# Shift rows summed before the mean square, 128-wide early products, and sliding-window values as float32 products at two column positions

## The chip, the core and the metric

The kernel runs on one core of a Trainium2 chip. A core has five engines that each work through their own list of instructions in order: TensorE (PE; its weight loads are listed apart as PEld), VectorE (DVE), ScalarE (ACT), GpSimd (POOL) and SyncE (SP, which here only issues DMAs). They meet through semaphores. TensorE writes to PSUM banks, the others read those and write to SBUF. The metric is the device time of one execution in microseconds. The program is one launch.

## The reference

One layer of a decoder trunk over 512 tokens of width 1024, in float32, with conditioning by a vector `c`:

```python
mod = silu(c) @ w_ada + b_ada                     # six rows: shift, scale, gate, twice
h = rmsnorm(x, norm1_g) * (1 + scale1) + shift1
qa, ka, va, qd, kd, vd, ga, gd = split(h @ w_in)
out_a = sliding_window_attention(qa, ka, va)      # 8 heads of 64, 2 key/value heads, window 128, sinks, ALiBi
out_d = diff_attention(qd, kd, vd)                # 4 heads, two softmax maps each, values 128 wide
merged = sigmoid(ga) * (out_a @ w_branch_swa) + sigmoid(gd) * (out_d @ w_branch_diff)
x = x + gate1 * (merged @ w_out)
h2 = rmsnorm(x, norm2_g) * (1 + scale2) + shift2
x = x + gate2 * conv_ffn(h2)                      # 2816 wide, causal conv of width 3, GELU, gate
return rmsnorm(x, final_g)
```

In the sliding-window attention the 512 queries are four blocks of 128, and a block sees its own block of keys and the one before. The probabilities of a head (a block of queries by up to 256 keys) are multiplied with the values of that head's key/value head.

## The kernel before

**Products in split form.** Most products are made from operands that are split into a high part in the type float32r and a low part, the remainder. `mm3` (line 105) issues three products: high by high, high by low and low by high. A split costs one copy on ScalarE (the high part) and one subtraction on VectorE (the low part); `split` (line 101) does it for weights, and `evac` (line 374) for results that leave PSUM. Products in plain float32 occur too: the column sums of squares, the sums of one modulation block, and the transposes and warming products against an identity or ones. A plain float32 product shows as two weight loads and two matmul records in the profile, a transpose as one of each.

**The start (lines 165 to 345).** VectorE, ScalarE, TensorE and GpSimd run in the order written (`manual_schedule`). SP loads x transposed in four pieces, then for each of eight blocks k of 128 features two blocks of modulation weights (`adaw[k]`, filled by `load_ada`, line 170) and a block of the input projection (`w0[k]`). For k = 0 the block in place j = 0 is laid out for TensorE (`w_ada_0`, the scale of the first 128 features); all others are rows for VectorE. `keep_warm` (line 205) issues products whose result nobody reads. The order for the first block is:

- ScalarE squares x in four pieces; VectorE adds the halves of a piece; `sums` (line 262) makes four products of a piece with a column of ones, `NB` = 48 columns wide, into one PSUM bank that a product with zeros has cleared.
- `rstd_start` (line 136) takes the mean square `ms` on VectorE and a power on GpSimd; `head_mod` (line 249) makes eight products for the scale, also `NB` wide; `mod_rows(0, 1)` sums the shift rows on VectorE (a multiplication with a running sum, line 232); `rstd_end` finishes `rst`, one over the root.
- two warming products, the high split of `w0[0]`, `mod_end` (line 234) on ScalarE, four transposes that spread `rst` (line 285), four warming products, and then x is scaled (line 292), h is formed (line 298) and the first products of the projection follow.

For each further block, 24 products of 512 columns run while VectorE and ScalarE make the next block's h.

**Sliding-window attention (lines 472 to 552).** The heads are taken in four pairs, head i with head i + 4; the two heads of a pair use different key/value heads. TensorE keeps its order as written; the other engines are ordered by a planner. For a pair there are `swa_scores` (two calls, products of 64 rows, the two heads in the two halves of the array's rows), `swa_softmax` (exponentials on ScalarE, scaling by one over the sum on VectorE, line 522), `swa_transpose` (line 524, one call for each head: seven transposes into two PSUM banks of the tag "t", each evacuated as a high and a low part) and `swa_values` (line 539). The value product is full width: `va` is held as high and low parts, with each key/value head's 64 columns in its own half of 128 and zeros in the other, so both heads add up into one bank `o`. `turn_va` (line 402) makes `va` from the transposed projection, after GpSimd has cleared it.

Between these calls `fill(n)` (line 431) issues n steps of other work for TensorE, the projections of later tiles; one step is three products of 512 columns. The counts stand in `SWA_FILL` and `DIFF_FILL`. A function handed to `after(n, ...)` runs n steps later. While the steps run, rows of the modulation for later use are loaded and summed on VectorE (`ada_rows`, line 679).

**Differential attention (lines 584 to 673)** follows, block by block for four heads, with `diff_values(h)` (line 643) one block into the next head, and for the last head after a `fill(1)` at line 792. `diff_values` reads the split transposed maps `aTh` and `aTl`; statistics and the scaling of its result come 10 and 26 steps later. Merge, output projection, MLP and final norm come behind, and no edit touches them.

Of the kernel before, what the change touches and what calls it, by code (L numbers as in the profile page):

```python
# [8 lines left out]
F32 = mybir.dt.float32  # L9
F32R = mybir.dt.float32r  # L10
# [4 lines left out]
P = 128  # L15
# [3 lines left out]
NT = S // P  # L19
# [24 lines left out]
def kernel(  # L44
# [60 lines left out]
    def mm3(o, lh, ll, rh, rl, start, stop):  # L105
        nc.tensor.matmul(o, lh, rh, start=start, stop=False)
        nc.tensor.matmul(o, lh, rl, start=False, stop=False)
        nc.tensor.matmul(o, ll, rh, start=False, stop=stop)
# [27 lines left out]
    def rstd_start(ssq, n, d, wpool, plus=None):  # L136
        ms = wpool.tile([P, n], F32, tag="rs_a", bufs=3, name="ms")
        if plus is None:
            nc.vector.tensor_scalar(ms, ssq, 1.0 / d, EPS, ALU.mult, ALU.add)  # L139
        else:  # L140
            nc.vector.scalar_tensor_tensor(ms, ssq, 1.0 / d, plus, ALU.mult, ALU.add)
        r0 = wpool.tile([P, n], F32, tag="rs_c", bufs=3, name="r0")
        nc.gpsimd.tensor_tensor(r0, ms, mhalf[:, :n], ALU.pow)  # L143
        return ms, r0
# [25 lines left out]
    def load_ada(k):  # L170
        if k % 4 < 2:
            adaw[k] = big.tile([P, 2, D], F32, tag=("outh", "outl")[k % 4], name=f"adaw{k}")
        else:
            adaw[k] = pp.tile([P, 2, D], F32, tag="adaw", bufs=2, name=f"adaw{k}")
        for j in range(2):
            src = w_ada_t[(1 - j) * D + k * P : (1 - j) * D + (k + 1) * P, :] if k or j else w_ada_0
            nc.sync.dma_start(adaw[k][:, j], src)

# [26 lines left out]
    def keep_warm(n):  # L205
        for i in range(n):
            nc.tensor.matmul(acc[5][:, :P], ones, ones, start=True, stop=True)
# [22 lines left out]
    def mod_rows(k, j):  # L230
        a = adaw[k][:, j]
        nc.vector.tensor_tensor_reduce(a, a, csb, 1.0, 0.0, ALU.mult, ALU.add, mods[k][:, 2 + j : 3 + j])
# [11 lines left out]
    def split_lo(k):  # L244
        nc.vector.tensor_sub(wts[k][1], w0[k], wts[k][0].bitcast(F32))

    NB = 48

    def head_mod():
        for a in range(KT):  # L250
# [3 lines left out]
            )  # L254

    stat = acc[6][:, : NT * NB].rearrange("p (t n) -> p t n", n=NB)
    zeros = pp.tile([P, NT * NB], F32, name="zeros")
    nc.gpsimd.memset(zeros, 0.0)
    keep_warm(2)
    nc.tensor.matmul(acc[6][:, : NT * NB], ones, zeros, start=True, stop=True)  # L260

    def sums(p):
        for t in range(NT):
            nc.tensor.matmul(
                stat[:, t], sqs[p][:, t * P : (t + 1) * P], ones[:, :NB], start=False, stop=True,
                skip_group_check=True,
            )

    sqs = [pp.tile([P, 2 * S], F32, tag="sq", bufs=4, name=f"sq{p}") for p in range(KT // 2)]
    for p in range(KT // 2):  # L270
        nc.scalar.activation(sqs[p], xT[:, p], AF.Square)
        if p == 1:
            nc.scalar.copy(csb[:, S:], acc[1])
        nc.vector.tensor_add(sqs[p][:, :S], sqs[p][:, :S], sqs[p][:, S:])
        sums(p)
    ms, r0 = rstd_start(stat[:, :, 0], NT, D, pp)
    head_mod()
    mod_rows(0, 1)
    rst = pp.tile([P, NT], F32, name="rst")
    rstd_end(rst, ms, r0, NT, pp)  # L280
    keep_warm(2)
    split_hi(0)
    mod_end(0, [acc[3][:, 0:1], mods[0][:, 3:4]])
    for t in range(NT):
# [74 lines left out]
    ddf = cpool.tile([P, 512], F32, name="ddf")  # L359
    nc.gpsimd.iota(ddf, [[1, 512]], base=-384, channel_multiplier=-1, allow_small_or_imprecise_dtypes=True)  # L360
    nc.gpsimd.affine_select(ddf, ddf, [[-1, 512]], ALU.is_ge, NEG, base=384, channel_multiplier=1)
    va = big.tile([P, 2, 4, 2 * P], F32R, tag="kvB", name="va")
    nc.gpsimd.memset(va.bitcast(F32), 0.0)
    man.close()
    p1.close()

# [7 lines left out]
    def evac(hi, lo, src, scale=None):  # L374
        if scale is None:
            nc.scalar.copy(hi, src)
            nc.vector.tensor_sub(lo, src, hi.bitcast(F32))
        else:
            nc.scalar.activation(hi, src, AF.Copy, scale=scale)
            nc.vector.scalar_tensor_tensor(lo, src, scale, hi.bitcast(F32), ALU.mult, ALU.subtract)  # L380
# [21 lines left out]
    def turn_va():  # L402
        pv = tbank("pva")
        for t in range(NT):
            nc.tensor.transpose(pv[:, t * P : (t + 1) * P], vaT[:, t * P : (t + 1) * P], ident)
        pv3 = pv.rearrange("p (t d) -> p t d", t=NT)
        for a, cc in ((0, 0), (64, 192)):
            evac(va[:, 0, :, cc : cc + 64], va[:, 1, :, cc : cc + 64], pv3[:, :, a : a + 64])

    with tc.issue_after(tiles[KT - 1, 0].ins):  # L410

# [19 lines left out]
    def fill(n):  # L431
        for _ in range(n):
            if not current:
                prefetch(2 if tick[0] else 1)
                if loaded:
                    wts, run = loaded.pop(0)
                    current.append(run(wts))
                    if tick[0]:
                        prefetch()
            if tick[0] in (2, 7):  # L440
                prefetch(1 if tick[0] == 2 else 2)
            if current:
                try:
                    next(current[0])
                except StopIteration:
                    current.clear()
            for e in list(later):
                e[0] -= 1
                if e[0] <= 0:
                    later.remove(e)  # L450
                    e[1]()
            tick[0] += 1
            if tick[0] >= ADA_START and tick[0] % ADA_EVERY == 0:
                next(ada, None)
# [68 lines left out]

    def swa_transpose(i, j):
        c = pairs[i]
        ph = ap.tile([P, 1024], F32R, tag="aTh", bufs=2, name=f"pTh{i}_{j}")
        pl = ap.tile([P, 1024], F32R, tag="aTl", bufs=2, name=f"pTl{i}_{j}")
        for b in range(2):
            wb = 512 if b == 0 else 384
            tp = tbank(f"tp{i}_{j}_{b}")  # L530
            for m in range(wb // P):
                kb, n = 2 * b + m // 2, 2 * b + m // 2 + m % 2
                off = (kb - max(0, n - 1)) * P
                nc.tensor.transpose(tp[:, m * P : (m + 1) * P], c.sb[n][:, j, off : off + P], ident)
            with tc.high_priority(offset=HP):
                evac(ph[:, b * 512 : b * 512 + wb], pl[:, b * 512 : b * 512 + wb], tp[:, :wb])
        c.pT.append((ph, pl))

    def swa_values(i):
        o = vbank(f"oa{i}")  # L540
        for j in range(2):
            ph, pl = pairs[i].pT[j]
            vs = slice(P * j, P * j + P)
            for kb in (0, 2, 1, 3):
                w = P if kb == 3 else 2 * P
                mm3(
                    o[:, kb * P : kb * P + w],
                    va[:, 0, kb, vs], va[:, 1, kb, vs],
                    ph[:, kb * 256 : kb * 256 + w], pl[:, kb * 256 : kb * 256 + w],
                    j == 0 and kb == 0, j == 1 and kb == 3,  # L550
                )
        evac(outa[0][:, i], outa[1][:, i], o)

# [235 lines left out]
            fill(DIFF_FILL[3])  # L789
    for j in range(6, KT):  # L790
        add_gate_a(j)
    fill(1)
    diff_values(DIFF_HEADS - 1)
    while units or loaded or current:
        fill(1)
# [935 lines left out]
```

## Time and profile before

| | |
|---|---|
| runs | 703.93, 704.18, 707.34 us (median 704.18) |
| profiled execution | 704.71 us, span 702.9 us |
| mean granted TensorE clock | 0.989 |
| busy: TensorE, weight loads | 684.5 us (97%), 601.4 us (86%) |
| busy: VectorE, ScalarE, GpSimd | 568.2 us (81%), 377.1 us (54%), 75.3 us (11%) |
| bytes moved by DMA | 119.68 MB, 170 GB/s |

All times are counted from the start of the span. The start runs to about 62 us, sliding-window attention from there to about 130, differential attention to about 231; the MLP's main products begin near 400. In a group row, "x24" is a count, then come the busy time, the mean length in ns, and the engine's idle time ahead of the group with what ended it. "A <- B" among the waits is an engine and line that waited, and the instruction that let it go on. The granted clock is 1.00 or 0.50 of full speed in this trace. Matmul records overlap, so a busy TensorE is not one at its peak rate: where a price is wanted, the distance from one start to the next is used.

### The profile page before, as it was taken

How to read it: one execution, taken by the hardware profiler on the slowest of the kernel's cores; microseconds unless marked ns; L12 is line 12 of the kernel's file. 1: busy time of each engine (PE TensorE's matmuls, PEld its weight loads, DVE VectorE, ACT ScalarE, POOL GpSimd, SP SyncE). 2: the span in 40 equal slices, each digit the busy share in tenths (PEclk: the TensorE clock that was granted, in tenths of full speed). 3: DMA queues.
4: the chain of work that ended last, by engine and by line, in shares of the span. 5: the costliest groups of instructions: out<-in, count | busy, mean ns of one | idle time of the engine just before them, and what ended most of it. 6: DMA issues, size and time to landing. Idle time of an engine off the chain costs nothing. (4 is left out here: it accounts for less than half of the span.)

```text
span 702.9 us, 11006 instructions
## 1 busy us (share of the span) xinstructions
PE 684.5 (97%) x4155; PEld 601.4 (86%) x4155; DVE 568.2 (81%) x1046; ACT 377.1 (54%) x662; POOL 75.3 (11%) x83
## 2 busy tenths in 40 slices
PE   8999899999998999999999999999999999999994
PEld 8887678877886788888889999999999998888873
DVE  3888999687787467673589898888888999979995
ACT  4656565454554243332478566655565665655663
POOL 3100000000010000000030111111101003431200
PEclk8999999999999999999999999999999999999998
DMA  9943453435364366239526888788777648996803
GB/s 356 397 162 112 152 152 120 122 120 160 110 180 150 123 210 213 102 102 269 180 57 153 197 196 204 171 223 191 185 182 194 151 166 195 197 204 178 154 1 120
DMA packets 71077, 119.68 MB, mean 170 GB/s; under 512 B 3952, under 2 KB 47728, under 8 KB 71024
## 3 DMA queue, kind: packets, MB, share of 16 engines
q1 hardware_dynamic: 52960, 95.04, 40.9%
q0 software_dynamic: 17776, 23.60, 20.4%
q8 instruction: 32, 0.52, 0.3%
q10 hardware_dynamic: 288, 0.34, 0.1%
q14 instruction: 21, 0.17, 0.1%
HBM read 116.87 MB, written 2.10 MB: 169 GB/s over the span
## 5 line engine op out<-in xcount | busy, mean ns | idle before, releaser
L1062 PE MATMUL up<-t,m_whi 128*128 128x256 f32 x528 | 96.1, 283 | 0.0
L1062 PEld LDWEIGHTS up<-t,m_whi 128*128 128x128 f32 x528 | 82.3, 192 | 0.0
L1062 PE MATMUL up<-t,m_wlo 128*128 128x256 f32 x264 | 74.7, 283 | 0.1
L1062 PE MATMUL up<-bh,p_wlo 128*128 128x256 f32 x232 | 65.7, 284 | 0.7 <-DVE p_wlo L1005 0.7
L1062 PE MATMUL up<-bh,p_whi 128*128 128x256 f32 x232 | 65.6, 283 | 0.0
L1062 PE MATMUL up<-bl,p_whi 128*128 128x256 f32 x232 | 65.6, 283 | 0.0
L684 DVE CUSTOM_DVE_ANT_0 ra<-ra,csb 128x1024 f32<-128x1024 f32 x32 | 39.1, 1223 | 24.3 <-DMA ra<-in_w_ada_t_dram 24.3
L1062 PEld LDWEIGHTS up<-t,m_wlo 128*128 128x128 f32 x264 | 50.6, 192 | 0.3 <-DVE m_wlo L1005 0.3
L1062 PEld LDWEIGHTS up<-bh,p_wlo 128*128 128x128 f32 x232 | 44.4, 192 | 1.1 <-DVE p_wlo L1005 1.1
L143 POOL TENSOR_TENSOR r<-ms,mhalf 128x1 f32<-128x1 f32 (+1 forms) x13 | 12.7, 979 | 303.2 <-DVE ms L139 227.0
L1062 PEld LDWEIGHTS up<-bh,p_whi 128*128 128x128 f32 x232 | 44.5, 192 | 0.0
L1062 PEld LDWEIGHTS up<-bl,p_whi 128*128 128x128 f32 x232 | 44.5, 192 | 0.0
L973 POOL DMA_DIRECT2D s<-in_w_up_dram x21 | 27.1, 1364 | 155.9 <-DMA s<-in_w_up_dram 110.9
L1005 DVE TENSOR_TENSOR m_wlo<-s,m_whi 128x1024 fp32r<-128x1024 f32 x31 | 37.8, 1219 | 2.0 <-ACT m_whi L1001 2.0
L1001 ACT CAST m_whi<-s 128x1024 fp32r<-128x1024 f32 x31 | 32.4, 1046 | 9.3 <-DVE s L995 6.0
L623 ACT ACTIVATE sd<-sd,dmx 128x128 f32<-128x128 f32 (+3 forms) x32 | 17.8, 557 | 30.8 <-DVE dmx L621 24.6
L1062 PE MATMUL up<-t,p_whi 128*128 128x256 f32 x176 | 32.2, 283 | 0.0
L1062 PEld LDWEIGHTS up<-t,p_whi 128*128 128x128 f32 x176 | 27.4, 192 | 0.2 <-issue 0.2
L1069 ACT ACTIVATE gT<-a,cols 128x512 f32<-128x512 f32 x22 | 17.7, 813 | 17.7 <-DVE a L1104 17.3
L1001 ACT CAST p_whi<-wa 128x1024 fp32r<-128x1024 f32 x18 | 18.7, 1041 | 12.0 <-DMA s<-in_w_up_dram 7.2
L1062 PE MATMUL up<-t,p_wlo 128*128 128x256 f32 x88 | 24.9, 283 | 0.0
L1005 DVE TENSOR_TENSOR p_wlo<-wa,p_whi 128x1024 fp32r<-128x1024 f32 x18 | 22.0, 1222 | 3.5 <-ACT p_whi L1001 3.0
(507 smaller groups left out, 2062.2 us busy)
## 6 DMA issues: line engine op xcount, KB each, us to landing
ra<-in_w_ada_t_dram SPq DMA_DIRECT2D x32, 512.0 KB, 3.3
wa<-in_w_up_dram SPq DMA_DIRECT2D x22, 512.0 KB, 4.7
s<-in_w_up_dram SPq DMA_DIRECT2D x21, 512.0 KB, 4.9
s<-in_w_up_dram POOLq DMA_DIRECT2D x21, 512.0 KB, 6.3
adaw<-in_w_ada_t_dram SPq DMA_DIRECT2D x15, 512.0 KB, 9.0
a<-in_w_up_dram SPq DMA_DIRECT2D x11, 512.0 KB, 4.6
b<-in_w_down_dram SPq DMA_DIRECT2D x10, 512.0 KB, 4.1
w<-in_w_first_dram SPq DMA_DIRECT2D x8, 512.0 KB, 9.9
```

What stands on the lines that cost most here:

```text
L143: nc.gpsimd.tensor_tensor(r0, ms, mhalf[:, :n], ALU.pow)
L623: nc.scalar.activation(pm[m], pm[m], AF.Exp, bias=mx[:, m : m + 1], scale=slope, accum_out=lsum[:, m : m + 1])
L684: nc.vector.tensor_tensor_reduce(r, r, csb, 1.0, 0.0, ALU.mult, ALU.add, late_mod[:, idx : idx + 1])
L973: nc.gpsimd.dma_start(dst, upblock(*blk), accum_op=ALU.add)
L1001: nc.scalar.copy(W[J, name][0], R[J, SRC[name]])
L1005: nc.vector.tensor_sub(lo, R[J, SRC[name]], hi.bitcast(F32))
L1062: nc.tensor.matmul(o[u], w[:, k, cu], b[:, k], start=name in ("p1", "m5", "p2") and k == 0 and x == 0, stop=k == 3 and x == 2, skip_group_ ...
L1069: nc.scalar.activation(grow(j), av[J][:, u], AF.Identity, bias=cv[:, 66 + j : 67 + j], scale=cv[:, 44 + j : 45 + j])
```

## The change

- `load_ada` issues the two loads of a block in the other order: the shift rows first, the scale block second.
- `NB` goes from 48 to 128, for the sums of squares and for `head_mod`. The product with zeros and its tile go; the first of the sums starts the bank.
- `mod_rows(0, 1)` moves ahead of `rstd_start`. The two warming products behind `rstd_end` go.
- `va` is one float32 tile without zeros, made by one ScalarE copy. GpSimd's clearing of it goes.
- `swa_transpose` evacuates into one float32 tile for each head, by ScalarE alone.
- `swa_values` makes one float32 product for each key block and head, 64 columns of weights each. The first head writes partitions 0 to 63 of the bank, the second 64 to 127.
- Ahead of the last `diff_values` there are four steps of filling in place of one.

```diff
-        for j in range(2):
+        for j in (1, 0):
             src = w_ada_t[(1 - j) * D + k * P : (1 - j) * D + (k + 1) * P, :] if k or j else w_ada_0
             nc.sync.dma_start(adaw[k][:, j], src)
...
-    NB = 48
+    NB = P
...
-    zeros = pp.tile([P, NT * NB], F32, name="zeros")
-    nc.gpsimd.memset(zeros, 0.0)
     keep_warm(2)
-    nc.tensor.matmul(acc[6][:, : NT * NB], ones, zeros, start=True, stop=True)
...
-                stat[:, t], sqs[p][:, t * P : (t + 1) * P], ones[:, :NB], start=False, stop=True,
+                stat[:, t], sqs[p][:, t * P : (t + 1) * P], ones[:, :NB], start=p == 0 and t == 0, stop=True,
...
+    mod_rows(0, 1)
     ms, r0 = rstd_start(stat[:, :, 0], NT, D, pp)
     head_mod()
-    mod_rows(0, 1)
     rst = pp.tile([P, NT], F32, name="rst")
     rstd_end(rst, ms, r0, NT, pp)
-    keep_warm(2)
     split_hi(0)
...
-    va = big.tile([P, 2, 4, 2 * P], F32R, tag="kvB", name="va")
-    nc.gpsimd.memset(va.bitcast(F32), 0.0)
+    va = big.tile([P, NT, P], F32, tag="kvB", name="va")
...
-        pv3 = pv.rearrange("p (t d) -> p t d", t=NT)
-        for a, cc in ((0, 0), (64, 192)):
-            evac(va[:, 0, :, cc : cc + 64], va[:, 1, :, cc : cc + 64], pv3[:, :, a : a + 64])
+        nc.scalar.copy(va.rearrange("p t d -> p (t d)"), pv)
...
-        ph = ap.tile([P, 1024], F32R, tag="aTh", bufs=2, name=f"pTh{i}_{j}")
-        pl = ap.tile([P, 1024], F32R, tag="aTl", bufs=2, name=f"pTl{i}_{j}")
+        pt = ap.tile([P, 1024], F32, tag=("aTh", "aTl")[j], bufs=2, name=f"pT{i}_{j}")
...
-                evac(ph[:, b * 512 : b * 512 + wb], pl[:, b * 512 : b * 512 + wb], tp[:, :wb])
-        c.pT.append((ph, pl))
+                nc.scalar.copy(pt[:, b * 512 : b * 512 + wb], tp[:, :wb])
+        c.pT.append(pt)
...
-        for j in range(2):
-            ph, pl = pairs[i].pT[j]
-            vs = slice(P * j, P * j + P)
-            for kb in (0, 2, 1, 3):
-                w = P if kb == 3 else 2 * P
-                mm3(
-                    o[:, kb * P : kb * P + w],
-                    va[:, 0, kb, vs], va[:, 1, kb, vs],
-                    ph[:, kb * 256 : kb * 256 + w], pl[:, kb * 256 : kb * 256 + w],
-                    j == 0 and kb == 0, j == 1 and kb == 3,
+        for kb in (0, 2, 1, 3):
+            w = P if kb == 3 else 2 * P
+            for j in range(2):
+                hd = slice(64 * j, 64 * j + 64)
+                nc.tensor.matmul(
+                    o[hd, kb * P : kb * P + w], va[:, kb, hd], pairs[i].pT[j][:, kb * 256 : kb * 256 + w],
+                    start=kb == 0, stop=kb == 3, skip_group_check=True,
                 )
...
     for j in range(6, KT):
         add_gate_a(j)
-    fill(1)
+    fill(4)
     diff_values(DIFF_HEADS - 1)
```

## The prediction

> **What bounds the kernel now.** I read the page first (engine totals), then the waits of the tensor engine, then granted clock by stretch, and last the timeline of the three places that the edits touch.
>
> ```profile
> span 702.9 us, 11006 instructions
> PE 684.5 (97%) x4155; PEld 601.4 (86%) x4155; DVE 568.2 (81%) x1046; ACT 377.1 (54%) x662; POOL 75.3 (11%) x83
> ```
>
> TensorE is the bound. The profiled execution took 704.71 us (span 702.9 and 1.8 around it); the median of the three runs shown is 704.18, half a microsecond less. I sum against 704.71. A microsecond counts if it is tensor work, a tensor wait, or tensor work at a low clock. What TensorE waits for between 18 and 354 us (columns: in total, times, longest):
>
> ```profile
> PE tp L534 <- DVE pTl L377: 2.6, 3, 1.9
> PE td L638 <- DVE sd L629: 1.9, 2, 1.2
> PE tp L534 <- DVE va L377: 0.7, 1, 0.7
> ```
>
> Two of the three wait for instructions that the change removes. The granted clock in stretches chosen to fit its steps (columns: stretch; then length, busy time and count of each engine, clock, DMA):
>
> ```profile
> 5.31:8.72 3.41, 2.77 (x23) 2.32 (x21) 2.79 (x10) 3.40 (x4) 0.00 (x0) 1.00 1.03 419
> 8.72:12.14 3.42, 3.42 (x34) 3.42 (x32) 1.64 (x4) 1.06 (x2) 0.00 (x0) 1.00 1.03 412
> 12.14:15.55 3.41, 3.41 (x18) 3.41 (x18) 1.59 (x5) 1.58 (x3) 2.96 (x10) 0.50 1.03 410
> 76.99:80.40 3.41, 1.56 (x13) 1.05 (x13) 3.41 (x9) 0.57 (x2) 0.00 (x0) 1.00 0.27 62
> 80.40:83.81 3.41, 3.41 (x18) 2.70 (x15) 3.41 (x12) 0.40 (x2) 0.00 (x0) 0.50 0.64 226
> ```
>
> The clock is halved twice near the edits, each time behind a stretch in which the array streamed little: 8.72 to 12.14 (busy throughout, but with products 48 wide) and 76.99 to 80.40 (1.56 us busy).
>
> **Part 1, the start.** (Timeline rows are start, length; the second row is one of a group: mean length in ns; the third: shortest, median and longest length, then first and last start.)
>
> ```profile
> 7.42 0.49 PE L260 MATMUL av<-zeros,ones 128*128 128x192 f32 x2
> L260 PE MATMUL av<-zeros,ones 128*128 128x192 f32 x2 | 0.5, 327 | 0.0
> L264 PE MATMUL av<-ones,sq x32: 275/275/310, 8.1 to 11.6; 128*128 128x48 f32 x32
> 9.89 0.69 DVE L274 TENSOR_TENSOR sq<-sq 128x512 f32<-128x512 f32 x1 [0.44 <-ACT sq L271]
> 11.69 3.20 PE L251 MATMUL av<-cs,adaw 128*128 128x48 f32 x16
> 11.89 0.16 DVE L139 TENSOR_SCALAR ms<-av 128x4 f32<-128x4 f32 x1 [1.30 <-PE av L264]
> 12.01 1.23 DVE L232 CUSTOM_DVE_ANT_0 adaw<-adaw,csb 128x1024 f32<-128x1024 f32 x1
> 14.55 0.16 DVE L153 SCALAR_TENSOR_TENSOR rst<-rt,r 128x4 f32<-128x4 f32 x1
> 15.67 1.06 PE L285 MATMUL av<-ident,rst 128*128 128x128 f32 x4
> 16.77 0.75 DVE L292 TENSOR_TENSOR xT<-xT,av 128x256 f32<-128x256 f32 x2 [2.05 <-PE av L285]
> 23.06 0.82 ACT L298 ACTIVATE hThA<-xT,mod 128x512 fp32r<-128x512 f32 x1
> 24.05 0.40 PE L309 MATMUL aka<-hThA,whi 128*128 128x512 f32 x1
> ```
>
> The records of L260 and L264 are two for a product. The order is sums, ms, POOL power, rst, four transposes (L285), scale of x, h, products. rst is ready at 14.71, but TensorE is at half clock: the 16 records of the head's modulation take 3.2 us (about 0.21 each at half clock, against 0.11 for one of the sums) and two warming products sit behind them, so the transposes start only at 15.67.
>
> Widening 48 to 128: a record of the sums, 48 wide, comes every (11.6 - 8.1)/31 = 0.11 us; one of a 128-wide warming product at full clock too, (0.61 - 0.28)/3 = 0.11 (first row below, with the same 0.28 for its last one's length). So width costs about nothing (0 to 0.2 us for 32) and streams 2.7 times the columns. I take it that the clock then stays up through 12.14.
>
> ```profile
> 6.97 0.61 PE L207 MATMUL ava<-ones 128*128 128x128 f32 x4
> 2.65 0.66 SPq L177 DMA_DIRECT2D adaw<-in_w_ada_dram  x1
> 3.36 0.45 SPq L177 DMA_DIRECT2D adaw<-in_w_ada_t_dram  x1
> adaw<-in_w_ada_dram SPq DMA_DIRECT2D x1, 512.0 KB, 7.4
> adaw<-in_w_ada_t_dram SPq DMA_DIRECT2D x1, 512.0 KB, 8.0
> ```
>
> The two first loads change places in SP's queue. They landed at 2.65 + 7.4 = 10.05 and 3.36 + 8.0 = 11.36. Now the shift rows come at 10.05 and the scale block at 11.36; everything behind them on SP keeps its place. The row sum moves ahead of ms on VectorE: 10.58 to 11.81, inside the idle 1.30 us that VectorE spends before ms; without that cover ms would come 1.23 us later. The head's products now wait for 11.36, and TensorE is with the sums until about 11.6 anyway. So ms stays at 11.9 to 12.0 and rst at 14.8. The head's products take 16 x 0.11 = 1.8 us, to 13.5; with the warming pair gone, the transposes wait for rst alone: 14.8, then 4 x 0.11 and 0.28 for the last one's length, scale of x at 15.5 instead of 16.77. Gain 1.3 us. The zero product (0.49 from 7.42, over before the first sums at 8.1) and the zero fills on POOL, for which nothing waits: nothing either way. The shift carries to the end of this stage, because h of the next block (23.06 + 0.82 = 23.88) is followed at once by its products (24.05), and both follow from the scale of x. Bounds: 0.4 (clock falls as before) to 1.6.
>
> **Part 2, sliding attention, waits and clock.** Splitting the probabilities leaves VectorE:
>
> ```profile
> L377 DVE TENSOR_TENSOR pTl<-tp,pTh 128x512 fp32r<-128x512 f32 (+1 forms) x16 | 9.2, 619 | 1.0 <-ACT pTh L376 1.0
> 75.16 1.07 DVE L522 TENSOR_SCALAR st<-st,lsum 128x128 f32<-128x128 f32 x4
> 76.90 0.39 PE L108 MATMUL pqa<-hThA,wqa_l 128*128 128x512 f32 x1
> 79.14 1.01 PE L534 MATMUL tp<-ident,st 128*128 128x128 f32 x7 [1.85 <-DVE pTl L377]
> ```
>
> 9.2 us of VectorE go, and the two passes for va; ScalarE's copies stay (two for va become one). A transposes' bank is then free after ScalarE's copy alone. Waits removed: 2.6 + 0.7 = 3.3 us, and with each a restart (79.14 - 76.90 is 2.24; without the wait of 1.85 and the 0.23 of the product ahead 0.16 is left), so 0.6 for four: 3.9. The wait at 79.14 is what starved the stretch 76.99 to 80.40; with 2 us of it gone, the halved stretch behind it goes too: 3.41 us at half rate lose 1.7 us of work. Together 5.6. What is late next: the normalised scores on VectorE and ScalarE's exponentials. At the second turn of the first pair normalising ends at 75.16 + 1.07 = 76.23, and TensorE, without the 0.7 + 0.2 ahead of it, would come at 77.1 - 0.9 = 76.2: no slack, so I keep 0.6 back: 5.0. Bounds 0 (another operand late in the same places) to 5.6; in the diff stage the 1.9 us on sd could shrink as well, which I count only in the range.
>
> **Part 3, the value products.**
>
> ```profile
> 85.40 0.28 PE L106 MATMUL oa<-pTh,va 128*128 128x256 f32 x1
> 88.15 0.44 PE L106 MATMUL pq<-hThA,w_h 128*128 128x512 f32 x1
> 65.47 0.39 PE L108 MATMUL pqa<-hThA,wqa_l 128*128 128x512 f32 x1
> 65.79 0.97 PE L113 MATMUL sw<-ka,qa 64*128 64x256 f32 x12
> 66.69 0.50 PE L106 MATMUL pqa<-hThA,wqa_h 128*128 128x512 f32 x1
> ```
>
> A call now has 24 products and takes 88.15 - 85.40 = 2.75 us. The new one has 8 float32 products; float32 shows two records each (16 sums, 32 records), so 16 records. No row has a 64-column float32 product. The nearest is the zero product: two records 192 wide in 0.49 us, 0.327 being one's own length, so 0.16 from one to the next, 0.85 ns a column; 256 wide is 0.22, 128 is 0.11. One after another: 12 x 0.22 + 4 x 0.11 = 3.08. If the two column halves run side by side, one record apart: 8 records, 1.53, and 0.22 = 1.75. Changing the array's shape costs about 0.3 a call: the score products (64 rows) start 0.32 after the product ahead where a 512-wide one takes 0.22, and again about 0.1 twice at the way out. So 2.07 or 3.38 a call against 2.75: over four calls -2.7 or +2.5. The row that decides is the scores': 12 products 64x256 come every (0.97 - 0.28)/11 = 0.06 us, while the 24 of a call, full arrays, come every 0.115; two half arrays do run at once. I take -2.7.
>
> The Trainium skill (TensorEngine Tiling, Key Properties) says that tiles load weights and multiply independently and that a change of tiling mode drains the array; the score rows agree with both for rows, and no run here shows columns. By the Trainium skill's page TensorE: Matmul & The Clock Gate, Part 3, three column tiles gave 2.38 instead of 3; at that share of the ideal the estimate for a call would be about 2.25 and the term -2.0.
>
> **Part 4, last values later.**
>
> ```profile
> 228.79 0.50 PE L106 MATMUL od<-aTh,vvh 128*128 128x512 f32 x1
> 229.73 0.50 PE L107 MATMUL od<-aTl,vvh 128*128 128x512 f32 x1 [0.45 <-DVE aTl L377]
> 252.00 0.62 ACT L102 CAST vvh<-of 128x512 fp32r<-128x512 f32 x1 [1.42 <-DVE of L669]
> L106 PE MATMUL pB<-vvh,wbd x32: 389/389/389, 260.9 to 314.6; 128*128 128x512 f32 x32
> ```
>
> The second product starts 0.94 after the first, where 0.22 is its work. Three more fill steps (9 products of 0.23, 2.1 us) ahead of it cover aTl, and their own weights are those of the tile in progress, already split: gain 0.7 to 0.9, I take 0.8. This head's values reach the merge three steps later: the split of 252.0 falls at about 254, and the merge first reads it in its fourth step, three steps of 0.7 after 260.9, so nothing waits. Lower bound 0.
>
> **Sum.** 704.71 - 1.3 - 5.0 - 2.7 - 0.8 = 694.9 us.
>
> **Rivals.**
> Columns in turn: the halves don't overlap. For it: no row shows columns, and float32 issues both records of one half before the other's. Against: the score rows. 704.7 - 1.3 - 5.0 - 0.8 + 2.5 = 700.1.
> Same waits under another name: a transpose waits for normalised scores or a ScalarE copy queued behind a weight cast. For: VectorE is busy 81% of the whole span, and ScalarE's exponentials stand between it and the transposes. Against: it loses over 9 us here. 694.9 + 5.0 = 699.9.
> Clock falls anyway at 12.14: the modulation stays at 0.21 a record, to 15.0; scale of x at 16.1, and the first products lose 0.2 more; gain 0.5, 695.7. For: TensorE was not idle there (3.42 of 3.42). Against: the stretch before, with 2.77 busy but wide records, kept the clock. The Trainium skill (TensorE: Matmul & The Clock Gate, Part 1) puts throttling down to an idle window, by which width would not matter and this rival would hold; the trace differs, since a stretch without idle time was followed by a halved clock.
> Slower: in the column shape no record overlaps the next, so each pays its whole length: 0.33 for 192 wide, hence 0.38 for 256 and 0.27 for 128, 12 x 0.38 + 4 x 0.27 + 0.3 = 6.0 a call, +12.9 over four. 704.7 - 7.1 + 12.9 = 710.5. It ends slower once a call takes more than 2.75 + (7.1 + 3.5)/4 = 5.4 us. Against: row halves overlap at full rate.
>
> **How the numbers follow.** Half a per cent, 3.5 us, is about what separates a change from none here: the three runs lie 703.93 to 707.34. Chances: forecast 0.55, clock rival 0.12, columns in turn 0.13, renamed waits 0.12, slower 0.08. The bound for faster is 700.7, so the two rivals at 700 are split: faster 0.82, same 0.10, slower 0.08. The likeliest case alone spans 692 to 697 (terms at their bounds). The range runs from 690.5 (all of 5.6, the 1.9 on sd, the start at 1.6, and shape changes that cost nothing, 1.3 less: 690.8) to 702 (a rival at 700 with the start at 0.4 and part 4 at nothing: 701.8).
>
> **What would show it.** Right: clock 1.00 from 6 to 16 us; L292 near 15.5; no wait of tp on VectorE; clock 1.00 from 76 to 84; a value call of 2.1 us with 16 records; no gap at od in the last head. Wrong: value calls over 3 us; a new wait of tp on st or pT; a halved stretch elsewhere, which costs 1.7 us each.

## The result, and the profile after

The changed kernel takes 694.12 us in the median of four runs (692.70 to 695.11); the kernel before, in four runs, 704.05 us (701.80 to 707.34). The ratio is 0.985, with a 95% interval of 0.981 to 0.990. Timed again, six runs with the kernel before beside them on the same chip, it took 693.98 us against 702.98, ratio 0.987 (0.984 to 0.990). The forecast was 694.9.

The head of the profile page of the changed kernel, to be held against the first two lines shown of before:

```profile
span 693.3 us, 10915 instructions
PE 676.6 (98%) x4117; PEld 591.5 (85%) x4117; DVE 559.9 (81%) x1028; ACT 376.6 (54%) x661; POOL 72.7 (10%) x81
```

TensorE lost 7.9 us of busy time; the other 1.7 us of the span are time in which it sat idle before. What TensorE waits for between 18 and 354 us (in total, times, longest):

```profile
PE tp L526 <- ACT pT L528: 1.1, 1, 1.1
PE td L627 <- DVE sd L618: 0.8, 1, 0.8
PE th L1146 <- DVE xn L1136: 0.7, 1, 0.7
PE sw L113 <- DVE mx L492: 0.6, 1, 0.6
PE aka L305 <- ACT hThA L294: 0.3, 1, 0.3
```

Both waits of the transposes on VectorE are gone, and the one on `sd` reads 0.8 instead of 1.9 (this is not a gain of the change, see the last values further down). Two are new in the sliding attention: the transposes wait for a copy on ScalarE, and the scores for a maximum on VectorE. The two stretches of before in which TensorE was first starved and then at half clock, and 56 us of the stage (the columns as in the rows of before, where these 56 us read 52.77 busy and a clock of 0.97):

```profile
76.99:80.40 3.41, 3.41 (x22) 2.51 (x20) 3.41 (x11) 0.14 (x1) 0.00 (x0) 1.00 0.48 161
80.40:83.81 3.41, 3.41 (x24) 2.50 (x23) 2.13 (x7) 3.07 (x14) 0.00 (x0) 1.00 0.64 195
...
62.00:118.00 56.00, 54.37 (x349) 41.96 (x348) 49.01 (x164) 35.72 (x108) 0.00 (x0) 1.00 0.45 142
```

TensorE is busy throughout where it had 1.56 of 3.41, and the clock stays at 1.00. The timeline of a value call, with the product ahead of it and the two behind:

```profile
107.20 0.39 PE L108 MATMUL pq<-hThB,w_l 128*128 128x512 f32 x1
107.52 1.73 PE L537 MATMUL oa<-pT,va 128*64 128x256 f32 x16
109.19 0.50 PE L106 MATMUL pq<-hThB,w_h 128*128 128x512 f32 x1
109.52 0.40 PE L107 MATMUL pq<-hTlB,w_h 128*128 128x512 f32 x1
```

From the first start to the last these are 2.32 us. The same call of before took, by its own timeline, 117.94 - 114.67 = 3.27:

```profile
114.67 0.39 PE L108 MATMUL pq<-hThB,w_l 128*128 128x512 f32 x1
...
117.94 0.39 PE L107 MATMUL pq<-hTlB,w_h 128*128 128x512 f32 x1
```

So a call saves 0.95 us, all changes of shape included, and four save 3.8. The start, in the repeat of the changed kernel (why that one stands below):

```profile
8.53 3.84 PE L261 MATMUL av<-ones,sq 128*128 128x128 f32 x32 [0.50 <-DVE sq L271]
12.21 1.95 PE L251 MATMUL av<-cs,adaw 128*128 128x128 f32 x16
14.41 0.65 PE L281 MATMUL av<-ident,rst 128*128 128x128 f32 x4 [0.25 <-DVE rst L153]
15.09 0.75 DVE L288 TENSOR_TENSOR xT<-xT,av 128x256 f32<-128x256 f32 x2 [0.74 <-PE av L281]
17.09 0.40 PE L305 MATMUL aka<-hThA,whi 128*128 128x512 f32 x1
```

GpSimd's power, which lies between the mean square `ms` and `rst`, in the kernel before and in this repeat:

```profile
12.21 1.92 POOL L143 TENSOR_TENSOR r<-ms,mhalf 128x4 f32<-128x4 f32 x1 [10.54 <-DVE ms L139]
```
```profile
12.73 1.03 POOL L143 TENSOR_TENSOR r<-ms,mhalf 128x4 f32<-128x4 f32 x1 [11.26 <-DVE ms L139]
```

In the kernel before, VectorE's row sum runs beside it (12.01 to 13.24); in the changed one that sum is over by then (10.95 to 12.17). All nine profiles of kernels with the row sum moved have 1.03 us here, all five without have 1.92 or 1.93. The prediction did not see this.

And the last head's values in the first profile, which follow each other without a gap:

```profile
221.20 0.39 PE L106 MATMUL od<-aTh,vvh 128*128 128x512 f32 x1
221.42 0.39 PE L107 MATMUL od<-aTl,vvh 128*128 128x512 f32 x1
```

**Where the time went.** I compared the starts of the same tensor instructions in the profiles, in microseconds later (+) or earlier (-) than before, and took the difference from one mark to the next. Both columns are held against one profile of before; how much that one alone can carry, the part on the start shows.

| stretch (its marks) | predicted | first profile | repeat |
|---|---|---|---|
| start, to the first scores of the sliding attention | -1.3 | -0.46 | -1.57 |
| sliding attention, to the first transposes of the differential one | -7.7 | -7.82 | -7.49 |
| differential attention, to its last transposes | in the range only | -1.23 | -1.14 |
| last values, to the next merge work | -0.8 | -0.95 | -0.95 |
| start of the MLP (its transposes `th`, first to last, some 346 to 360 us) | 0 | +0.84 | +0.13 |
| rest | 0 | +0.01 | +0.37 |
| span | -9.8 | -9.61 | -10.65 |

### The profile page after: what moved, and what is told of

It is laid out like the page before. It is cut to its first block, busy times and chain, and to the rows that moved or that the text cites. A ratio compares the mean times of both kernels' runs of the same rounds, so it can differ in the third digit from the quotient of the medians.

```text
span 693.3 us, 10915 instructions
## 1 busy us (share of the span) xinstructions
PE 676.6 (98%) x4117; PEld 591.5 (85%) x4117; DVE 559.9 (81%) x1028; ACT 376.6 (54%) x661; POOL 72.7 (10%) x81
```

## The experiments

Every time below is a median of 5 to 12 runs, with 9 to 23 of the kernel before on the same chip in the same set; a ratio is to that one, with its 95% interval. The sets ran on different chips, so across sets the ratios are compared. First comes the changed kernel itself, then its parts, then the causes.

**The changed kernel again.** No edit.

> The changed kernel unaltered, on the chip of this set, as the measure for the others: 0.9855 of the kernel before.

693.98 us, before 702.98, ratio 0.987 (0.984 to 0.990). The table's last column is its profile. The start gained 1.57 there and 0.46 in the first one. What differs is the speed of the first products: four transposes of the conditioning columns

```profile
6.46 1.08 PE L218 MATMUL aka<-ident,cs 128*128 128x128 f32 x4 [0.70 <-DVE cols L222]
...
9.05 4.41 PE L261 MATMUL av<-ones,sq 128*128 128x128 f32 x32
...
6.83:10.24 3.41, 3.41 (x18) 3.41 (x17) 2.12 (x4) 2.65 (x4) 0.00 (x0) 1.00 1.02 412
```
```profile
6.53 0.62 PE L218 MATMUL aka<-ident,cs 128*128 128x128 f32 x4 [1.08 <-DVE cols L222]
```

take 1.08 us in the first profile (first fence) and 0.62 in the repeat (second), and the first profile's sums begin at 9.05 instead of 8.53 and last 4.41 instead of 3.84. In it the records come every 0.21 us until 10.37 us and every 0.11 behind. The granted clock of that stretch (third row) reads 1.00 only because the view prints 1.00 where the trace has no entry: the trace's list of granted clocks begins, with 1.00, at 10.39 us in the first profile and at 4.96 in the repeat, and in each the distance of the records halves there. Counted back from this entry in steps of 3.41 us, the clock rose in all 14 profiles at the end of the first step in which TensorE was busy for 2.82 us or more; steps with 2.72 (the first profile, from 3.57) and 2.78 did not raise it. Twelve profiles have the entry between 3.95 and 6.71 us, two at 10.4. The same kernel runs both ways, so the size of this term can't be read from one profile. The Trainium skill (TensorE: Matmul & The Clock Gate, Part 1) says that the clock's window runs freely and that one kernel's slow first products therefore differ from run to run; these two profiles agree with that, 10.39 against 4.96.

**The start alone.** The kernel before, with the edits of the start.

```diff
-        for j in range(2):
+        for j in (1, 0):
...
-    NB = 48
+    NB = P
...
-    nc.tensor.matmul(acc[6][:, : NT * NB], ones, zeros, start=True, stop=True)
...
+    mod_rows(0, 1)
     ms, r0 = rstd_start(stat[:, :, 0], NT, D, pp)
     head_mod()
-    mod_rows(0, 1)
...
-    keep_warm(2)
```

> The kernel before with the edits of the start alone (order of the two loads, 128-wide products, no zero product, row sum ahead of ms, no warming pair). My prediction: 1.3 us off, about 702.8, with the clock at 1.00 from 6 to 19 us and the scale of x at 15.5. What the trace of the changed kernel suggests: the head start was 0.46 us when the first block's sums began at half clock, so the gain depends on where the clock's window falls in an execution and lies between 0.4 and 1.3. Rival: nothing is left of it at the end of the start, 704.1.

701.54 us, before 703.35, ratio 0.9974 (0.9963 to 0.9986), which is -1.8 us. In its profile the clock was never halved, and the first scores come 1.89 earlier. Over the profiles of all runs the first scores come at 62.1 to 64.6 us with the old start (five, mean 63.2) and at 60.4 to 62.2 with the new one (eight, mean 61.1).

This profile also shows how little one profile can carry. From the first scores to the first transposes of the differential attention it takes 70.6 us, where before takes 72.8 and the kernel with the later last values, two parts further down, 72.2. All three have the same instructions there, in the same order on VectorE. TensorE waits here for the same low parts (2.8 us, longest 2.1), but the clock stays at 1.00: these waits do not always bring a halved stretch.

**The values alone.** The kernel before, with the edits of `va`, `swa_transpose` and `swa_values`.

> The kernel before with the sliding-attention edits alone (va, transposes, values). The ladder of the two traces gives 7.8 us from 62 to 120 us and 1.3 more before the last transposes of the differential attention: 695 to 696.5. My prediction's two terms give 7.7. If the waits that went were owed to the earlier start of the stage, less than 6 is left, above 698.

697.81 us, before 703.35, ratio 0.9923 (0.9903 to 0.9943), -5.4 us (-4.0 to -6.8): less than the 7.7 of the prediction's two terms, and less than the comparison of the profiles had promised. The stage gained 6.1 in its profile, the end 7.0.

**The later last values alone.**

```diff
-    fill(1)
+    fill(4)
     diff_values(DIFF_HEADS - 1)
```

> The kernel before with four fill steps in place of one ahead of the last values. Prediction 0.8 us, ladder of the traces 0.95: about 703.2, and the gap of 0.45 at od gone. Rival: the statistics of the last head come later and hold up the merge or the MLP's start: 704 or more.

701.72 us, before 703.35, ratio 0.9985 (0.9971 to 0.9999), -1.1 us; in the profile the step itself brings -0.94, and no gap is left. The three parts add up to 8.3 us by their ratios, the whole change to 10.3 and 9.2 in its two measurements. The intervals are 0.8 to 3 us wide to either side, so they neither show nor exclude that the parts depend on each other by a microsecond or two.

**Only the subtractions gone.** The kernel before, its 24 products for a call kept. It leaves out the low part of the probabilities and takes the high part a second time, so its result is not the layer's.

```diff
-                evac(ph[:, b * 512 : b * 512 + wb], pl[:, b * 512 : b * 512 + wb], tp[:, :wb])
+                nc.scalar.copy(ph[:, b * 512 : b * 512 + wb], tp[:, :wb])
-        c.pT.append((ph, pl))
+        c.pT.append((ph, ph))
```

> The kernel before without the VectorE subtraction of the transposed probabilities; the second of the three value products takes the high part again, so the low part of the probabilities is left out of the result and a call keeps its 24 products and 2.75 us. If VectorE's load sets the pace of this stage, nearly the whole gain of the sliding-attention edits stays: 697 to 699 against 697.8 of those edits alone (703.4 before). If the shorter call made it, no more than 3 us are gained, above 700.

699.26 us, before 703.06, ratio 0.995 (0.993 to 0.997), -3.8 us. The sliding attention alone shortens by 4.6 in its profile (the start came late in that one, with the clock at half until 10.4 us). What TensorE still waits for there:

```profile
PE tp L533 <- DVE va L377: 0.5, 1, 0.5
PE sw L113 <- DVE mx L499: 0.3, 1, 0.3
```

The 2.6 us on the low parts are gone, and so is the halved clock. This is the term "waits and clock" by itself, but for the wait on `va`, of which 0.5 stays.

**The short value calls, the subtractions put back.** The changed kernel, with VectorE subtracting the copy from the bank into a tile that nobody reads.

```diff
                 nc.scalar.copy(pt[:, b * 512 : b * 512 + wb], tp[:, :wb])
+                spare = ap.tile([P, 512], F32, tag="spare", bufs=1, name=f"spare{i}_{j}_{b}")
+                nc.vector.tensor_sub(spare[:, :wb], tp[:, :wb], pt[:, b * 512 : b * 512 + wb])
```

> The changed kernel with the VectorE subtractions of the transposed probabilities put back, into a tile that nobody reads: the value products stay 16 float32 records, but VectorE has its 9 us again and a transposes' bank is held until the subtraction is done. If the waits of the transposes were owed to these subtractions, they come back: 3 to 4.5 us over the changed kernel, and a wait of tp on VectorE line 377 or its like. If the shorter value call alone made the gain, it stays within 1 us of the changed kernel.

702.69 us, before 702.98, ratio 0.998 (0.996 to 1.000): 8.7 us above the changed kernel, where 3 to 4.5 were expected. The waits of TensorE in the stage, and the stretches around the two halved ones:

```profile
PE tp L526 <- DVE spare L530: 6.3, 7, 2.1
```
```profile
75.42:78.83 3.41, 1.57 (x13) 1.17 (x15) 3.41 (x6) 0.92 (x2) 0.00 (x0) 1.00 0.41 154
78.83:82.25 3.42, 3.42 (x17) 2.62 (x14) 3.42 (x12) 0.15 (x1) 0.00 (x0) 0.53 0.51 171
...
106.00:109.40 3.40, 1.29 (x7) 0.60 (x5) 3.40 (x10) 0.64 (x2) 0.00 (x0) 1.00 0.26 102
109.40:112.80 3.40, 3.33 (x18) 2.63 (x19) 3.40 (x8) 0.48 (x1) 0.00 (x0) 0.55 0.46 155
```

The value calls are as short as in the changed kernel, and their 3.8 us gain nothing: the stage takes 0.8 us longer in this profile than in that of before. VectorE is busy in all of 75.42 to 78.83 and 106.00 to 109.40, TensorE waits for it 6.3 us instead of 2.6 (and 0.7 on `va`), and the clock is halved twice instead of once. The planner also gave VectorE another order than in the kernel before, so how much of the 6.3 comes from TensorE's coming sooner and how much from that order is open.

The two terms of my sum are not independent. One makes TensorE faster in the stage; only the other lets it use that. On top of the relief the short calls are worth 5.4 - 3.8 = 1.6 us of time (6.1 - 4.6 = 1.5 in the stage of the two profiles), not 3.8; the intervals of the two times are some 1.4 us to either side.

**The two halves of the columns in turn.** The changed kernel, head after head.

```diff
-        for kb in (0, 2, 1, 3):
-            w = P if kb == 3 else 2 * P
-            for j in range(2):
-                hd = slice(64 * j, 64 * j + 64)
+        for j in range(2):
+            hd = slice(64 * j, 64 * j + 64)
+            for kb in (0, 2, 1, 3):
+                w = P if kb == 3 else 2 * P
```

> The changed kernel with the loops of the value products exchanged: all key blocks of the first head, then all of the second, so that neighbours sit at the same column position. If the gain of the call is the overlap of the two column halves, a call grows from 1.67 to about 3.2 us (16 records of 0.22 and 0.11 in turn) and the kernel by 6 us, to 700. If a call is short for another reason (fewer products, or records that overlap within one half), it stays at 694.

695.53 us, before 703.35, ratio 0.990 (0.988 to 0.992): 1.5 us above the changed kernel, 2.2 by the two ratios, and far less than expected. A call takes 2.58 us, by the third one's row and the start of the next product:

```profile
107.40 2.65 PE L537 MATMUL oa<-pT,va 128*64 128x256 f32 x16
109.98 0.50 PE L106 MATMUL pq<-hThB,w_h 128*128 128x512 f32 x1
```

By the starts of the single records of the first call, the second head's first one begins at 80.164, before the first head's sixth at 80.374, though all eight of the first head stand ahead of it in the list. So even in turn the halves overlap by about 0.65 us. Four calls 0.91 longer are 3.6 us, of which the stage keeps only 1.5 to 1.8: it waits for nothing that the view of the waits lists, where the changed kernel waited 1.7. The later TensorE arrives, the less of these waits there is.

**The early products 48 wide.** The changed kernel with one number undone.

```diff
-    NB = P
+    NB = 48
```

> The changed kernel with 48 columns in place of 128 for the sums and the modulation. By the theory that the clock's window counts streamed columns, the clock falls to 0.50 during the start again, the modulation's records come every 0.21 us, and the kernel loses 0.5 to 1.5 us. By the rival that only idle time counts, it keeps 1.00 and the time.

694.15 us, before 702.98, ratio 0.987 (0.984 to 0.989), the same as with 128. Its profile shows the clock as I had argued; first this kernel, then the repeat of the changed one, in the same stretches:

```profile
9.27:12.68 3.41, 3.41 (x33) 3.41 (x32) 2.52 (x5) 0.93 (x1) 0.14 (x1) 1.00 1.03 414
12.68:16.09 3.41, 3.41 (x19) 3.41 (x19) 0.84 (x5) 1.58 (x3) 2.87 (x13) 0.53 1.02 407
16.09:19.50 3.41, 3.41 (x13) 2.93 (x12) 2.95 (x6) 3.22 (x5) 1.94 (x2) 0.50 1.03 411
```
```profile
9.27:12.68 3.41, 3.41 (x33) 3.41 (x33) 2.65 (x5) 1.04 (x1) 0.00 (x0) 1.00 1.02 413
12.68:16.09 3.41, 3.02 (x26) 2.64 (x24) 1.49 (x6) 2.06 (x4) 2.82 (x12) 1.00 1.03 413
```

Equally many records, equally busy; behind the narrow ones the clock is halved for two stretches (0.53 because it fell at 12.91), behind the wide ones not. In all six profiles with products 48 wide, this one and the five with the old start, the clock is halved once in the start; in none of the eight with 128 it is. Here it costs 1.40 us at the first products and 0.95 at the first scores. But at the end only 0.17 of it is left, for the stage that follows then waits 0.2 on the scores where the repeat waits 0.9. Here, too, what the start gains is partly waited away later. The Trainium skill (TensorE: Matmul & The Clock Gate, Part 1) has the clock fall after an idle window of some 3.4 us; the length agrees (the clock is halved here for 3.41, 6.83 or 10.24 us), the rows do not agree with "idle", since TensorE worked in all of 9.27 to 12.68.

**VectorE relieved in the kernel before.** While the attention runs, VectorE also sums rows of the modulation. Here they begin 24 steps later.

```diff
-ADA_START = 16
+ADA_START = 40
```

> The same shift of the modulation rows in the kernel before. VectorE loses about 4.9 of 62 us in the sliding attention and the subtractions stay. If VectorE's load is what holds up TensorE, half of the waits go: 2 to 4 us under the kernel before. If it is the hold on the transposes' banks by the subtraction alone, less than 1 us.

705.01 us, before 703.06, ratio 1.003 (1.001 to 1.005): no gain, and the same wait, longer:

```profile
PE tp L534 <- DVE pTl L377: 4.1, 2, 3.1
```

What VectorE does ahead of the longest wait, in the kernel before and here:

```profile
77.25 1.22 DVE L684 CUSTOM_DVE_ANT_0 ra<-ra,csb 128x1024 f32<-128x1024 f32 x1
...
78.39 1.15 DVE L377 TENSOR_TENSOR pTl<-tp,pTh 128x512 fp32r<-128x512 f32 x2
```
```profile
77.38 1.22 DVE L684 CUSTOM_DVE_ANT_0 ra<-ra,csb 128x1024 f32<-128x1024 f32 x1
...
78.53 0.69 DVE L377 TENSOR_TENSOR pTl<-tp,pTh 128x512 fp32r<-128x512 f32 x1
```

ScalarE's copy of the bank was done at 75.70 and 77.18. Then the subtraction that frees the bank stood behind scores and a row sum of 1.22 us. The edit took three of ten row sums out of the stage, but not this one. So less load in the stage was not enough; the wait goes by what stands ahead of the subtraction in VectorE's order. Whether it goes when this one row sum is moved was not tried.

**VectorE relieved in the changed kernel.** The same edit on the changed kernel, and then (the edit shown) with the rows closer together, one every 6 steps, so that the last comes no later than in the changed kernel.

```diff
-ADA_EVERY = 7
+ADA_EVERY = 6
...
-ADA_START = 16
+ADA_START = 40
```

> The changed kernel with the sums of the later modulation rows started at step 40 in place of 16, which takes about four of their ten 1.22 us passes on VectorE out of the sliding attention. If VectorE still sets the pace there, the two waits left in it (0.9 and 1.0) go: 1 to 2 us under the changed kernel. If TensorE is the bound by now, no change; if the rows come to stand in the differential attention's way, 1 us over.

> The changed kernel with the modulation rows started at step 40 as in the run before, but one row every 6 steps, so that the last is made at step 232 and not later than in the changed kernel itself. Theory (the 2.5 us that the later rows gained in the sliding attention were given back because the rows then reached into the merge and the start of the MLP): the stage's gain stays, the waits at the merge and the MLP's start are those of the changed kernel, about 691.5, 0.983 of before. Rival (VectorE and ScalarE have no room for denser rows in the differential attention, or the give-back has nothing to do with the rows): waits of TensorE on VectorE between 130 and 250, or the same loss behind 270, 694 or more, 0.987 or above.

692.95 us, before 703.06, ratio 0.986 (0.983 to 0.988), and 693.92 us, before 703.35, ratio 0.985 (0.983 to 0.988): neither is told apart from the changed kernel. In the stage both gain, 10.0 us over before where the changed kernel had 7.5 to 7.8, and no wait of TensorE is left in it (the row is the first one's; the second has 56.00 busy, too). The other three rows are from the second, further on:

```profile
62.00:118.00 56.00, 56.00 (x368) 43.27 (x367) 46.45 (x157) 37.03 (x109) 0.00 (x0) 1.00 0.39 123
```
```profile
PE th L1146 <- DVE xn L1136: 2.0, 1, 2.0
```
```profile
342.10:345.50 3.40, 1.44 (x8) 0.92 (x7) 2.54 (x8) 0.72 (x2) 0.94 (x1) 1.00 0.00 0
345.50:348.90 3.40, 3.40 (x13) 2.87 (x13) 2.60 (x7) 2.91 (x8) 0.34 (x1) 0.56 0.00 0
```

It is given back at the start of the MLP by a wait of 2.0 us on the normalised rows and a halved stretch behind it. My first reason, that the later rows reach into that place, holds for 1.1 us alone, a wait on a modulation row in the first kernel that is gone in the second. The second, whose rows end early, still loses 3.1 us at the MLP's start. There a load of weights arrives later (rows of ScalarE's cast that waits for it: changed kernel, rows closer):

```profile
335.90 1.05 ACT L1188 CAST early<-wa 128x1024 fp32r<-128x1024 f32 x1 [1.42 <-DMA wa<-in_w_up_dram]
```
```profile
334.16 1.05 ACT L1188 CAST early<-wa 128x1024 fp32r<-128x1024 f32 x1 [2.73 <-DMA wa<-in_w_up_dram]
```

SP issues that load at 330.32 and 327.28, so it took 5.6 and 6.9 us, and 4.9 in the repeat. The cast is followed on VectorE by the low part, which sits ahead of the sums that end in the normalised rows. In all 14 profiles the two go together: the transposes `th` take 13.1 to 13.3 us from first to last where the cast starts up to 4.9 us after the issue, 13.4 to 14.0 with 5.0 to 5.6, and 16.5 and 16.6 in the two kernels with later rows, with 6.9 each. The bytes moved in the window 326 to 336 of the last kernel (forty slices of 0.25 us):

```profile
GB/s 238 315 336 307 336 336 344 373 365 360 324 295 311 311 381 385 295 143 70 53 29 25 25 25 25 25 20 25 25 20 16 102 160 266 348 340 389 344 127 16
```

Nearly all of it has moved by 331; then for more than 2 us some 25 GB/s trickle in, about a sixteenth of 370, and the packets of that time take 7.0% of sixteen engines, about one engine's time. So one DMA engine of sixteen is late, and the cast starts only behind it. The Trainium skill (DMA: Bandwidth & Descriptors, the section on why a DMA adds 16 to its semaphore) says that the engines of a transfer finish independently; this row agrees. Whether the later rows make that engine late, or it is chance, two profiles don't settle: in the twelve others the cast starts 4.1 to 5.6 us after the issue.

**Filling moved within the pairs.** One step of filling from the last place of `SWA_FILL` to the fifth, to give the transposes' copies more time, and two more warming products at the start.

```diff
-SWA_FILL = (0, 3, 6, 2, 2, 2, 2, 3)
+SWA_FILL = (0, 3, 6, 2, 3, 2, 2, 2)
...
-    keep_warm(10)
+    keep_warm(12)
```

> The changed kernel with one step of filling moved from behind the value products to between the two transposes of a pair, and twelve warming products at the very start in place of ten. The moved step should cover the two waits that are new in the trace after (0.57 before the fourth pair's second scores, 1.06 before its second transposes): 1.2 to 1.8 us off. The two warming products close the idle 0.9 us ahead of the first spread, which kept the clock at half until about 10 us: 0 to 0.8 us off. Together 1.2 to 2.6 under the changed kernel. Rival: the waits only move to the values or the next scores, no change.

696.50 us, before 702.98, ratio 0.990 (0.987 to 0.992), 2.5 us above the changed kernel, where 1.2 to 2.6 below were expected. The wait moved, and drew a halved stretch after it:

```profile
PE pk L106 <- DVE qa L375: 2.2, 1, 2.2
```
```profile
88.50:91.90 3.40, 1.18 (x8) 0.97 (x8) 3.40 (x12) 1.42 (x2) 0.00 (x0) 1.00 0.85 225
91.90:95.30 3.40, 3.40 (x20) 2.67 (x19) 2.03 (x7) 1.07 (x2) 0.00 (x0) 0.52 0.45 154
```

A projection now waits for a subtraction on VectorE (the low part of `qa` in `evac`), and VectorE is busy in all of the 3.40 us. Which of the two edits did it was not separated.

## Why the prediction was right

The time came out 0.8 us from the forecast, and the mechanisms named were at work. That the sum is so near is partly luck: several sizes were off by about a microsecond, in both directions.

- **Start, -1.3 predicted.** By the timed part -1.8, in the repeat's profile -1.57, in the first one -0.46. The head's products come at 0.11 each (1.95 us with the last one's length), the transposes 0.22 behind `rst`, the clock is at 1.00, and the scale of x comes at 15.09 where I had 15.5. One step was not as I had it. I kept the distance from `ms` to `rst`: `ms` at 11.9 to 12.0, `rst` at 14.8. In the repeat `ms` came at 12.41, half a microsecond later, since the sums lasted to 12.4, and `rst` still began at 14.19 where it began at 14.55 in the kernel before. The distance is 1.78 us where it was 2.66, by the power on GpSimd, 1.03 instead of 1.92. So moving the row sum brought 0.9 us that I had put at nothing, the late `ms` took 0.5 of it back, and the shorter way from `rst` to the scale of x brought 1.3, as predicted. What I had also not seen is that a run can keep half pace up to 10.4 us, and that the next stage waits part of a gain here away: of 0.95 at its beginning 0.17 was left at the end.
- **Waits and clock in the sliding attention, -5.0 predicted.** Alone it is 4.6 in the stage, 3.8 in the timed ratio. If all of the 3.8 us of shorter calls is taken off the stage's gain, 7.82 - 3.8 = 4.0 is left in the first profile and 7.49 - 3.8 = 3.7 in the repeat. Part of the term, the halved stretch, does not always come with these waits, as the start alone shows. The step that was too small is what I kept back for "what is late next", 0.6. Next were a ScalarE copy of the transposes, 1.1, and a maximum ahead of the scores, 0.6 to 0.9. ScalarE's timeline shows the first as I had described it in the rival of renamed waits, a copy queued behind a weight cast:

```profile
114.51 1.04 ACT L102 CAST wba_h<-wba 128x1024 fp32r<-128x1024 f32 x1
115.45 0.96 ACT L528 COPY pT<-tp 128x512 f32<-128x512 f32 x2
```

That rival was thus true for about 1 us, not for 5.

- **Value calls, -2.7 predicted; the calls themselves are 3.8 us shorter.** The halves of the columns run side by side, as the score rows had suggested for rows. I had counted one record's time before the second half joins and 0.3 for changes of shape, 2.07 a call. But the records start in pairs, 6 to 7 ns apart, from the first: 12 records of 256 columns come at 0.216 a pair. Two halves here reach the full factor: a pair takes 0.216, and with the columns in turn one such record alone takes 0.216 as well. By the Trainium skill's page TensorE: Matmul & The Clock Gate, Part 3, where three column tiles gave 2.38 instead of 3, the term would have been -2.0, an estimate.
- **Not additive.** My sum treated the two as separate. The short calls without the freed VectorE gained nothing, and made the stall worse. On top of the relief they were worth 1.6 of their 3.8. A sum over terms of one stage holds only as long as the engine next to the bound keeps up. Against the profile of before, 7.5 to 7.8 of the predicted 7.7 came, because the error of one term and that of the other cancelled, 1.0 to 1.3 too much and 1.1 too little; timed alone it was 5.4. The profile of before has the longest stage of the three with the same instructions there, so that agreement is luck.
- **Last values, -0.8 predicted,** -0.95 in both profiles and -0.94 alone. The wait on `sd`, which I counted in the range only, reads 1.1 less, and the table has 1.1 to 1.2 for its stage. That is not a gain of the change: the kernel with the later last values, whose instructions up to there are those of before, waits 0.8 on `sd` and takes 91.1 us from the first to the last transposes, like the changed kernel, where the one profile of before takes 92.4. The start of the MLP took 0.1 to 0.8 back, through the late load.
- **Rivals.** Columns in turn: refuted by the pairs. Clock falls anyway: refuted by the pair of kernels 48 and 128 wide and by all eight profiles with 128, though it would have made no difference to the time beyond the interval. Same waits under another name: true for about 1 us, as said. Slower, by records that don't overlap: refuted, a call takes 1.67 us.

## What to carry to other kernels

When a change speeds up the bounding engine and relieves its neighbour in the same stage, price the two together: put the relief back into the fast version once, and you see whether the speed alone is worth anything (here 3.8 us of shorter calls were worth nothing by themselves, and about 1.6 with the relief). A wait on an engine that is mostly idle or mostly busy says little by that engine's load; look at what stands ahead of the releasing instruction in its order. And where a stage still has waits, microseconds gained ahead of it, or taken out of it, return in part at the next wait. A comparison by stages needs more than one profile of the kernel before: the one used here was 0.7 to 2.3 us longer in one stage, and 0.5 to 1.3 in the next, than two kernels with the same instructions there.

## What the runs showed of the hardware that was not expected

- Products for different column halves of the array can overtake the order of the list: with eight records of one half listed ahead, the other half's first began 0.21 us ahead of the sixth of them. The Trainium skill (TensorE: Matmul & The Clock Gate, Part 3, on the mechanism) says that products keep their order of start; by these records that does not hold across column halves.
- The clock fell after a stretch in which TensorE was busy all the time with 48-wide products, and not after an equal one with 128-wide ones. Elsewhere it fell after stretches with 1.18, 1.29, 1.44 and 1.57 of 3.4 us busy. It first rose behind a step of 3.41 us with at least 2.82 busy, and not behind 2.72 or 2.78.
- A power over 128 by 4 numbers on GpSimd took 1.92 us while a row sum ran on VectorE and 1.03 without it (five and nine profiles). What the two engines share here, the profiles do not show.
- A load can be complete but for about one DMA engine's share, which trails by 2 us at about 25 GB/s; nothing in the view of the waits tells this from a load that was slow as a whole, the slices of the DMA do.
